# Latent queries from six column blocks, with the rotated rows carried to their heads

## The chip, the cores and the metric

One Trainium2 chip, one of its cores. The metric is the device time of one execution in microseconds (us). The kernel before took 927.07 us, the median of three runs (926.96 to 927.24).

## The reference, cut to what matters

One layer of an encoder on 512 tokens of width 1024: a SwiGLU block, a mixer, a SwiGLU block, each between RMS norms. The mixer runs neighbourhood attention (8 heads of 64) and latent attention (8 heads) over one input projection. The change touches the latent attention's queries and keys alone:

```python
q = (rms_norm(c_q, q_norm_g) @ w_uq).reshape(B, S, H, 64 + 32)
q_nope, q_rot = jnp.split(q, [64], axis=-1)
q_rot = apply_rope(q_rot, cos, sin)      # x1*cos - x2*sin, x2*cos + x1*sin
k_rot = apply_rope(k_rope, cos, sin)     # one key part, shared by the heads
s = (q_nope . k_nope + q_rot . k_rot) * 96 ** -0.5
```

The latent `c_q` has 256 columns, so a query product contracts over two blocks of 128. Each head has 64 columns without position and 32 with it, the latter in two halves x1 and x2 of 16.

## The kernel before

All products run as three matmuls over float32r halves: `mm3` (line 353) takes hi.hi, hi.lo and lo.hi, where `split` (line 333) makes hi by a copy on ACT (ScalarE) and lo by a subtraction on DVE (VectorE), or on POOL (GpSimd) where that is asked for. PE is TensorE, SP is SyncE, which issues most DMAs in the order of the program; POOL issues a few.

The whole layer is written as calls that only collect operations (`Plan`, line 44). `issue` (line 220) then orders all of them, for all engines, once at build time, from costs and due times that `add` and `place` hold, and writes them out in that order. So on the chip each engine has a fixed order, and a wait holds up what stands behind it on its engine.

The mixer's part that matters here, in the order of the source:

- `na_pair` (line 996) does the neighbourhood attention for two heads at a time; its output stands in `ov`, the right half of `h[1]`, its values V in columns 8192 to 12287 of the big region.
- `latent(n)` (line 1085) makes the latents of token tile n, normalises them and builds the rotated key. In columns 384 to 511 of `cb[n]` stand the products with cos, the products with sin, and their sum twice (line 1108). `latent_T` (line 1110) transposes the tile, and `split` writes `cT`; its block 3 has the rotated key in rows 64 to 127, twice the same 32 rows.
- `q_weights(u)` (line 1142) loads the query weights of four heads into a raw buffer of 1024 columns: per head and block 64 + 32 columns and the 32 with position once more with their halves exchanged, by three DMAs. `q_head(hd)` (line 1149) makes a head's query as one product with 128 columns, so the array is full: 64 rows without position, 32 rotated, 32 exchanged. One DVE multiplication by `tbl` (line 1157) puts the scale on the first 64 rows, scale x cos on the next 32 and scale x sin with its signs on the last 32; `split` then writes the query's place (`Q_AT`, line 931). Each score's product with the doubled key rows adds the two parts.
- `k_pair(j)` (line 1178) makes the keys without position of two heads, `rope_rows(hd)` (line 1170) carries rows 64 to 127 of the rotated key to the buffers of heads 1 to 7 by DMAs within SBUF, issued by POOL.
- `mla_pair(j, hf)` (line 1187) does the attention of two heads for half of the tokens: scores, row minima on DVE, exponentials on ACT, transposes, a split into the probability buffers `pts` (line 1227: two of 2048 columns at 8192 and 10240, where V stood), products with the values. `w_out_a` (line 1230), the output projection of the neighbourhood half, is PE work that the plan may put in between.

PSUM has eight banks; `prep` (line 1081) hands out banks 0 to 5 in turn to the transposes, value, query and key products. The scores then use banks 0 and 1, the transposes 2 and 3 (line 1225). Raw weights have three buffers (line 285), split weights four (lines 286 and 287), both used in turn: the query weights of the two halves and the four of w_out's first half follow each other in them.

Of the kernel before, what the change touches and what calls it, by code (L numbers as in the profile page):

```python
# [14 lines left out]
AF = mybir.ActivationFunctionType  # L15
ALU = mybir.AluOpType
AX = mybir.AxisListType

P = 128
D = 1024  # L20
S = 512
# [6 lines left out]
EPS = 1e-6  # L28
NH = 8
TAIL = 3  # L30


class Ring:
# [10 lines left out]
class Plan:  # L44
# [3 lines left out]
    ahead, margin = 250, 0  # L48
    TAIL = {"ACT": 95, "DVE": 75, "POOL": 45, "PE": 176}
    LAG = {"ACT": 60, "DVE": 50, "POOL": 85, "PE": 120, "SP": 60}  # L50
# [60 lines left out]
    def add(self, eng, op, a, k):  # L111
# [16 lines left out]
        in_sb = sum(kind(x) != "psum" for x in big)  # L128
        tail, lock, dma = self.TAIL.get(eng, 0), False, 0
        if op == "dma_start":  # L130
# [111 lines left out]
def r_(ap):  # L242
    return ap.bitcast(F32R)
# [3 lines left out]
def hybrid_block(ctx, tc, A, out):  # L247
    nc = tc.nc
    plan = Plan(tc)
    ACT, DVE, POOL, PE, SP = (plan.engine(e) for e in ("ACT", "DVE", "POOL", "PE", "SP"))  # L250
# [13 lines left out]
    def bank(i, n=512):  # L264
        return psum[:, i * 512 : i * 512 + n]
# [31 lines left out]
    gbs = Ring([gbuf[:, :1024], gbuf[:, 1024:]])  # L297
    hall = new(4096)
    h = [hall[:, n * 1024 : (n + 1) * 1024] for n in range(NT)]
    tbl = h[3][:, 512:]  # L300
    mask = h[2][:, 512:768]
    tts = [new(1024)]
    R0 = at[1]
# [1 line left out]
    def reg(o, n):  # L305
        assert R0 + o + n <= NCOL - N32
        return mem[:, R0 + o : R0 + o + n]
# [25 lines left out]
    def split(dst_hi, dst_lo, src, eng=DVE):  # L333
        ACT.copy(r_(dst_hi), src)
        n = src.shape[-1]
        for c in [slice(i, i + 512) for i in range(0, n, 512)] if eng is POOL else [slice(0, n)]:
            eng.tensor_tensor(r_(dst_lo[..., c]), src[..., c], dst_hi[..., c], ALU.subtract)
# [6 lines left out]
    def load_w(src, n=1024, eng=DVE, raw=None, to=None):  # L344
        raw = fetch(src, n) if raw is None else raw
        hi, lo = to or (his.get()[:, :n], los.get()[:, :n])
        split(hi, lo, raw, eng)
        return hi, lo
# [4 lines left out]
    def mm3(ps, a, b, start, stop):  # L353
        mm(ps, a[0], b[0], start, False)
        mm(ps, a[0], b[1], False, False)
        mm(ps, a[1], b[0], False, stop)
# [37 lines left out]
    def ffn(w_gu, w_dn, gpost, on_tile, L, first, resid, mid_tile=None, rs=None):  # L394
# [134 lines left out]
        c0, n_pairs, n_first = L["pairs"]  # L529
        plain = [c for c in range(NFC - TAIL) if not c0 <= c < c0 + 2 * n_pairs]  # L530
        three = [reg(L["slots"][0], 1024), his.items[3], los.items[3]]
        slots = {c: three[i % 3] for i, c in enumerate(plain)}
        slots |= {c: reg(o, 1024) for c, o in zip(range(NFC - TAIL, NFC), L["slots"][1:])}
        w_to = {c: (his.items[i % 4], los.items[i % 4]) for i, c in enumerate(plain)}
# [262 lines left out]
    for k in range(KD):  # L797
        o = sq.get() if k else acc
# [14 lines left out]
    v = [x.rearrange("p (n t) -> p n t", n=NT) for x in (sq.items[0], bank(3))]  # L813
# [65 lines left out]
    def nb():  # L879
        return prb.get()  # L880
# [11 lines left out]
    for n in range(NT):  # L892
        ps = bank(2 * n)
# [37 lines left out]
    Q_AT = (7168, 5120, 18432, 19456, 20480, 4096, 6144, 25600)  # L931
# [27 lines left out]
    def o_rstd(g, ns):  # L959

        b = bank(trb.get(), 8)
        w = 2 * len(ns)
        for i, v in enumerate((sqs[g], sqr)[: g + 1]):
            for n, t in enumerate(ns):
                PE.matmul(b[:, 2 * n : 2 * n + 2], v[:, t * P : (t + 1) * P], ones, start=i + n == 0,
                          stop=i == g, skip_group_check=True)
        s = stat.get()[:, :w]
        DVE.tensor_scalar(s, b[:, :w], 1.0 / 512, EPS, ALU.mult, ALU.add)
        r = ors[g][:, 2 * ns[0] : 2 * ns[0] + w]
        POOL.tensor_tensor(r, s, nhalf.to_broadcast([P, w]), ALU.pow)  # L970
        return ors[g][:, ::2]
# [94 lines left out]
    qk_pair(2)  # L1066
    na_pair(2)
    qk_pair(3)
    SP.dma_start(tbl, A["tbl"])
    SP.dma_start(tokt.rearrange("p n c -> p (n c)"), A["tokt"])  # L1070
    na_pair(3)
    rA = o_rstd(0, range(NT))


    gc = (gbuf[:, 1792:], h[2][:, 768:896])
    v = A["g_c"]
# [4 lines left out]
    prep = Ring(list(range(6)))  # L1081
    cT = reg(14336, 4096).rearrange("p (a b t) -> p a b t", a=2, b=4)
    cTh = [cT[:, 0, i, :] for i in range(4)]
    cTl = [cT[:, 1, i, :] for i in range(4)]
    def latent(n):
        ps = bank(nb(), 416)
        for k in range(KD):
            w = [a.rearrange("p (k c) -> p k c", k=2)[:, k % 2, :] for a in wc[k // 2]]
            mm3(ps, xt(k, n * P, (n + 1) * P), w, k == 0, k == KD - 1)
        s = stat.get()  # L1090
        ACT.activation(cb[n][:, :256], ps[:, :256], AF.Square, scale=1.0 / 16, accum_out=s[:, 0:1])
        ACT.activation(cb[n][:, 256:384], ps[:, 256:384], AF.Square, scale=128.0 ** -0.5, accum_out=s[:, 1:2])
        DVE.tensor_scalar(s[:, 2:4], s[:, 0:2], EPS, None, ALU.add)
        r = stat.get()
        POOL.tensor_tensor(r[:, 0:2], s[:, 2:4], nhalf.to_broadcast([P, 2]), ALU.pow)
        r1, r2 = r[:, 0:1], r[:, 1:2]
        c = cb[n]
        DVE.scalar_tensor_tensor(c[:, 0:256], ps[:, 0:256], r1, gc[0], ALU.mult, ALU.mult)
        DVE.scalar_tensor_tensor(c[:, 256:384], ps[:, 256:384], r2, gc[1], ALU.mult, ALU.mult)
        tk = tokt[:, n, :]  # L1100
        DVE.tensor_tensor(c[:, 384:416], ps[:, 384:416], tk[:, 0:32], ALU.mult)
        v = ps[:, 400:416]
        v = bass.AP(tensor=v.tensor, offset=v.offset, ap=[v.ap[0], [-16, 2], [1, 16]])
        DVE.tensor_tensor(c[:, 416:448].rearrange("p (a c) -> p a c", a=2), v,
                          tk[:, 32:64].rearrange("p (a c) -> p a c", a=2), ALU.mult)
        v = [bass.AP(tensor=x.tensor, offset=x.offset, ap=[x.ap[0], [0, 2], [1, 32]])
             for x in (c[:, 384:416], c[:, 416:448])]
        DVE.tensor_tensor(c[:, 448:512].rearrange("p (a c) -> p a c", a=2), v[0], v[1], ALU.add)

    def latent_T(n):  # L1110
        b = bank(prep.get())
# [10 lines left out]
    raw = raws.get()  # L1122
# [16 lines left out]
    Q = {}  # L1139
    wq = {}  # L1140

    def q_weights(u):
        raw = raws.get()
        to, src = raw.rearrange("p (i c) -> p i c", i=8), A["w_uq"][u].rearrange("p (i c) -> p i c", i=8)
        for o, c0, c1 in ((0, 0, 96), (96, 80, 96), (112, 64, 80)):
            SP.dma_start(to[:, :, o : o + c1 - c0], src[:, :, c0:c1])
        wq[u] = [x.rearrange("p (k h c) -> p k h c", k=2, h=4) for x in load_w(None, raw=raw)]

    def q_head(hd):
        hi, lo = wq[hd // 4]  # L1150
        i = hd % 4
        ps = bank(prep.get())
        for k in range(2):
            mm3(ps, (hi[:, k, i, :], lo[:, k, i, :]), (cTh[k], cTl[k]), k == 0, k == 1)
        q = reg(Q_AT[hd], 1024)
        Q[hd] = (q[:, :512], q[:, 512:])
        DVE.tensor_tensor(ps, ps, tbl, ALU.mult)
        split(q[:, :512], q[:, 512:], ps)

    q_weights(0)  # L1160
    q_weights(1)
    for hd in range(NH):
        q_head(hd)
    kbuf = [(cTh[3], cTl[3])]
    for o in range(4):
        m = reg(21504 + 1024 * o, 1024)
# [222 lines left out]
```

## Time and profile before

| | |
|---|---|
| median of three runs | 927.07 us (926.96 to 927.24) |
| the profiled execution, its own time | 926.21 us |
| its span, first to last instruction | 924.1 us |
| mean granted TensorE clock | 0.998 of full |
| PE busy | 914.2 us, 99% of the span |
| DVE busy | 813.0 us, 88% |
| ACT busy | 544.1 us, 59% |
| POOL busy | 357.3 us, 39% |

The profile is of one execution. Busy times are sums over an engine's instructions, so they say how full an engine is over the whole span, not which one sets the time of a stage. PE counts as busy while a matmul's modelled length runs, and matmuls overlap; the distance between starts is the better measure of what one costs. Nearly every operation is written out by line 238, at the end of the planner, so a line tells nothing; operations are told apart by engine, shape and place in time. `m` is ordinary SBUF, `memr` the float32r region.

### The profile page before, as it was taken

Reading aid. Unit: us, or ns where it says so; the run is one execution under the profiler, and the core shown is the slowest. Engines: PE = TensorE matmul, PEld = TensorE weight load, DVE = VectorE, ACT = ScalarE, POOL = GpSimd, SP = SyncE. Lnnn points to the kernel's source line nnn. Section 1 sums busy time; section 2 is a strip of 40 time slices with the busy share of each in tenths; the row PEclk is TensorE's granted clock in tenths of the full one; section 3 lists DMA queues with packets and bytes.
Section 4 is the critical chain, followed back from the end, with each engine's and each line's share of the span. In section 5 each row is a group of like instructions: output and inputs, shape, how many; then the busy total and the mean of one; then the engine's idle time right before and its main releaser. Section 6 shows DMA issues by size and latency. Waiting matters only on the chain. (4 is left out here: it accounts for less than half of the span.)

```text
span 924.1 us, 15672 instructions
## 1 busy us (share of the span) xinstructions
PE 914.2 (99%) x5822; PEld 826.6 (89%) x5822; DVE 813.0 (88%) x1205; ACT 544.1 (59%) x972; POOL 357.3 (39%) x300
## 2 busy tenths in 40 slices
PE   9999999999999999999999999999999999999996
PEld 7889999999887788888978888999999999988785
DVE  7999999899999896588796678999998989999986
ACT  7446544544675674588777867655544444458562
POOL 0005777860300313222552323238787665130040
PEclk9999999999999999999999999999999999999999
DMA  7535354446534496314290115244434445464324
GB/s 259 171 114 183 115 145 142 158 124 221 171 126 149 114 268 181 63 57 93 93 190 26 46 46 180 94 171 162 144 119 144 131 126 180 142 208 145 114 69 159
DMA packets 65932, 128.02 MB, mean 139 GB/s; under 512 B 22337, under 2 KB 32449, under 8 KB 65857
## 3 DMA queue, kind: packets, MB, share of 16 engines
q1 hardware_dynamic: 64704, 125.20, 43.5%
q0 software_dynamic: 1008, 1.84, 1.2%
q8 instruction: 45, 0.74, 0.3%
q14 instruction: 31, 0.25, 0.1%
q10 hardware_dynamic: 144, 0.00, 0.0%
HBM read 107.36 MB, written 17.83 MB: 135 GB/s over the span
## 5 line engine op out<-in xcount | busy, mean ns | idle before, releaser
L238 PE MATMUL psum<-memr 128*128 128x256 f32 (+3 forms) x5480 | 894.0, 323 | 0.7 <-ACT memr L238 0.2
L238 PEld LDWEIGHTS psum<-memr 128*128 128x128 f32 x5480 | 788.4, 190 | 79.9 <-DVE memr L238 3.8
L238 POOL TENSOR_TENSOR m<-m 128x512 f32<-128x512 f32 (+7 forms) x255 | 318.1, 1263 | 491.5 <-DVE m L238 201.8
L238 ACT CAST memr<-m 128x1024 fp32r<-128x1024 f32 (+3 forms) x388 | 304.5, 811 | 223.8 <-PE psum L238 91.4
L238 DVE TENSOR_TENSOR memr<-m,memr 128x1024 fp32r<-128x1024 f32 (+4 forms) x379 | 405.0, 1098 | 17.8 <-ACT memr L238 16.9
L238 DVE TENSOR_TENSOR m<-psum,m 128x512 f32<-128x512 f32 (+4 forms) x199 | 125.0, 632 | 32.9 <-ACT m L238 22.6
L238 DVE TENSOR_TENSOR m<-m 128x512 f32<-128x512 f32 (+3 forms) x179 | 101.2, 589 | 3.6 <-DMA m<-in_ffn_w_down 0.5
L238 ACT CAST memr<-psum 128x512 fp32r<-128x512 f32 (+2 forms) x124 | 63.6, 522 | 31.2 <-PE psum L238 22.5
L238 DVE TENSOR_TENSOR memr<-psum,memr 128x512 fp32r<-128x512 f32 (+3 forms) x116 | 67.9, 603 | 12.5 <-ACT memr L238 11.3
L238 ACT COPY m<-psum 128x512 f32<-128x512 f32 (+3 forms) x98 | 45.4, 474 | 37.0 <-PE psum L238 34.6
L238 PE MATMUL psum<-m 128*128 128x128 f32 (+1 forms) x342 | 54.6, 279 | 2.1 <-DVE m L238 2.0
L238 DVE TENSOR_TENSOR psum<-psum,m 128x256 f32<-128x256 f32 (+1 forms) x86 | 49.9, 585 | 4.7 <-PE psum L238 3.1
L238 PEld LDWEIGHTS psum<-m 128*128 128x128 f32 x342 | 43.6, 155 | 10.0 <-DVE m L238 2.2
L238 ACT ACTIVATE m<-m 128x256 f32<-128x256 f32 (+3 forms) x88 | 41.4, 475 | 11.7 <-DVE m L238 11.5
L238 ACT ACTIVATE m<-psum 128x256 f32<-128x256 f32 (+2 forms) x62 | 27.4, 443 | 27.2 <-DVE psum L238 15.0
L238 DVE SCALAR_TENSOR_TENSOR m<-m 128x512 f32<-128x512 f32 (+1 forms) x36 | 32.2, 934 | 3.7 <-POOL m L238 3.2
L238 ACT ACTIVATE m<-psum,m 128x512 f32<-128x512 f32 x40 | 26.9, 687 | 7.7 <-DVE m L238 5.8
L238 POOL TENSOR_TENSOR memr<-m,memr 128x512 fp32r<-128x512 f32 (+1 forms) x14 | 23.2, 1673 | 14.1 <-ACT memr L238 7.7
L238 ACT ACTIVATE memr<-m 128x512 fp32r<-128x512 f32 (+2 forms) x28 | 20.9, 757 | 13.1 <-DVE m L238 11.6
L238 DVE TENSOR_REDUCE m<-psum 128x1 f32<-128x512 f32 x32 | 21.2, 682 | 2.0 <-PE psum L238 1.9
L238 ACT COPY psum<-m 128x512 f32<-128x512 f32 x28 | 16.3, 589 | 10.3 <-DVE m L238 10.0
L238 POOL CAST memr<-memr 64x512 fp32r<-64x512 f32 x8 | 5.9, 739 | 35.6 <-DVE memr L238 34.2
(26 smaller groups left out, 99.1 us busy)
## 6 DMA issues: line engine op xcount, KB each, us to landing
m<-in_ffn_w_gu SPq DMA_DIRECT2D x86, 512.0 KB
m<-in_ffn_w_down SPq DMA_DIRECT2D x44, 512.0 KB
gd<-m SPq DMA_DIRECT2D x44, 256.0 KB
m<-gd SPq DMA_DIRECT2D x64, 128.0 KB
m<-in_w_qk SPq DMA_DIRECT2D x8, 512.0 KB
h<-m SPq DMA_DIRECT2D x8, 512.0 KB
m<-in_w_out SPq DMA_DIRECT2D x8, 512.0 KB
m<-h SPq DMA_DIRECT2D x8, 512.0 KB
```

The lines of the kernel that those rows point to most:

```text
L238: r = getattr(self.engines[eng], op)(*a, **k)
```

## The change

- The query weights are loaded in another order, by two DMAs for each half of the heads: first the columns without position, 64 per head and block, then those with position, 32 per head and block; 768 columns, nothing doubled.
- `q_heads(u)` makes the queries of four heads from three column blocks of 128: one block holds the columns with position of all four heads, the two others those without position of two heads each. So there are six blocks in place of eight.
- The block with position is multiplied by cos (`cos4`) and by sin (`sin4`), each to a bank of its own, both are split into a spare region (columns 8192 to 12287, the later `pts`), and sixteen DMAs on SP carry 32 rows each to rows 64 to 95 and 96 to 127 of the heads' queries.
- The blocks without position are scaled on their way out of PSUM: ACT writes hi with the scale, DVE lo in one fused operation, over 64 rows per head.
- The exchange of the halves is now done on the key: the sum of the two products is written once, and a small DVE copy writes its exchanged form beside it.
- The table of 128 rows gives way to two: cos, repeated four times by one DMA, and sin, by eight DMAs of 16 rows into the right half of `h[1]`, after `na_pair(3)`.

```diff
+Q_SCALE = -(96.0 ** -0.5)
...
-    tbl = h[3][:, 512:]
+    cos4, sin4 = h[3][:, 512:], h[1][:, 512:]
...
-    SP.dma_start(tbl, A["tbl"])
+    v = A["tbl"]
+    SP.dma_start(cos4, bass.AP(tensor=v.tensor, offset=v.offset + 64 * S, ap=[[0, 4], [S, 32], [1, S]]))
     SP.dma_start(tokt.rearrange("p n c -> p (n c)"), A["tokt"])
     na_pair(3)
+    for i in range(8):
+        o = (112, 96)[i % 2] * S
+        SP.dma_start(sin4[16 * i : 16 * i + 16], bass.AP(tensor=v.tensor, offset=v.offset + o, ap=[[S, 16], [1, S]]))
...
-        v = [bass.AP(tensor=x.tensor, offset=x.offset, ap=[x.ap[0], [0, 2], [1, 32]])
-             for x in (c[:, 384:416], c[:, 416:448])]
-        DVE.tensor_tensor(c[:, 448:512].rearrange("p (a c) -> p a c", a=2), v[0], v[1], ALU.add)
+        DVE.tensor_tensor(c[:, 448:480], c[:, 384:416], c[:, 416:448], ALU.add)
+        v = c[:, 496:512]
+        v = bass.AP(tensor=v.tensor, offset=v.offset, ap=[v.ap[0], [-16, 2], [1, 16]])
+        DVE.tensor_copy(v, c[:, 448:480].rearrange("p (a c) -> p a c", a=2))
...
     def q_weights(u):
         raw = raws.get()
-        to, src = raw.rearrange("p (i c) -> p i c", i=8), A["w_uq"][u].rearrange("p (i c) -> p i c", i=8)
-        for o, c0, c1 in ((0, 0, 96), (96, 80, 96), (112, 64, 80)):
-            SP.dma_start(to[:, :, o : o + c1 - c0], src[:, :, c0:c1])
-        wq[u] = [x.rearrange("p (k h c) -> p k h c", k=2, h=4) for x in load_w(None, raw=raw)]
+        src = A["w_uq"][u].rearrange("p (i c) -> p i c", i=8)
+        for o, c0, c1 in ((0, 0, 64), (512, 64, 96)):
+            SP.dma_start(raw[:, o : o + 8 * (c1 - c0)].rearrange("p (i c) -> p i c", i=8), src[:, :, c0:c1])
+        wq[u] = load_w(None, 768, raw=raw[:, :768])
-    def q_head(hd):
...
+    def q_heads(u):
+        for i in range(4):
+            q = reg(Q_AT[4 * u + i], 1024)
+            Q[4 * u + i] = (q[:, :512], q[:, 512:])
+        def product(o, step):
+            ps = bank(prep.get())
+            for k in range(2):
+                mm3(ps, [x[:, o + step * k : o + step * k + P] for x in wq[u]], (cTh[k], cTl[k]), k == 0, k == 1)
+            return ps
+        ps, p2 = product(512, P), bank(prep.get())
+        DVE.tensor_tensor(p2, ps, sin4, ALU.mult)
+        DVE.tensor_tensor(ps, ps, cos4, ALU.mult)
+        for a, x in enumerate((ps, p2)):
+            m = reg(8192 + 2048 * u + 1024 * a, 1024)
+            split(m[:, :512], m[:, 512:], x)
+            for i in range(4):
+                q = reg(Q_AT[4 * u + i], 1024)
+                SP.dma_start(q[64 + 32 * a : 96 + 32 * a], m[32 * i : 32 * i + 32])
+        for j in range(2):
+            ps = product(P * j, 256)
+            for e in range(2):
+                hi, lo = (x[0:64] for x in Q[4 * u + 2 * j + e])
+                x = ps[64 * e : 64 * e + 64]
+                ACT.activation(r_(hi), x, AF.Copy, scale=Q_SCALE)
+                DVE.scalar_tensor_tensor(r_(lo), x, Q_SCALE, hi, ALU.mult, ALU.subtract)
...
-    for hd in range(NH):
-        q_head(hd)
+    for u in range(2):
+        q_heads(u)
```

## Rows read from the trace of the kernel before

**Rows 1.** The page: its span, and its first part, busy time by engine.

```profile
span 924.1 us, 15672 instructions
...
PE 914.2 (99%) x5822; PEld 826.6 (89%) x5822; DVE 813.0 (88%) x1205; ACT 544.1 (59%) x972; POOL 357.3 (39%) x300
```

**Rows 2.** Windows: length; busy PE, PEld, DVE, ACT, POOL (instructions); PE clock; DMA share; GB/s.

```profile
460.00:480.00 20.00, 20.00 (x89) 15.94 (x88) 18.62 (x30) 14.21 (x24) 13.18 (x14) 1.00 0.90 186
480.00:540.00 60.00, 59.98 (x366) 51.48 (x366) 43.69 (x82) 48.15 (x106) 18.74 (x19) 1.00 0.18 57
540.00:600.00 60.00, 58.79 (x389) 52.43 (x388) 49.90 (x71) 39.24 (x73) 16.62 (x17) 1.00 0.33 115
800.00:924.10 124.10, 116.79 (x533) 95.47 (x531) 108.21 (x170) 68.36 (x112) 22.85 (x33) 0.98 0.41 131
466.50:474.00 7.50, 7.50 (x35) 6.21 (x34) 7.29 (x13) 5.31 (x9) 2.68 (x3) 1.00 1.17 191
```

**Rows 3.** Waits of PE, whole span: total us, times, longest.

```profile
PE psum L238 <- DVE m L238: 2.0, 3, 1.1
```

**Rows 4.** Timeline of DVE from 463.9 to 485: start, length (both us), what.

```profile
463.96 0.69 DVE L238 TENSOR_TENSOR psum<-psum,m 128x512 f32<-128x512 f32 x1
...
465.91 1.29 DVE L238 TENSOR_TENSOR psum<-psum,m 128x512 f32<-128x512 f32 x2
...
480.06 1.28 DVE L238 TENSOR_REDUCE m<-psum 128x1 f32<-128x512 f32 x2
```

**Rows 5.** Groups by shape, 457.5 to 481.5: count | busy us, mean ns | idle before.

```profile
L238 PE MATMUL psum<-memr 128*128 128x512 f32 x101 | 24.2, 397 | 0.0
...
L238 DVE TENSOR_TENSOR memr<-psum,memr 128x512 fp32r<-128x512 f32 x16 | 10.4, 682 | 0.9 <-ACT memr L238 0.7
L238 ACT CAST memr<-psum 128x512 fp32r<-128x512 f32 x15 | 8.8, 587 | 6.3 <-DVE psum L238 4.7 <-PE psum L238 1.2
L238 DVE TENSOR_TENSOR psum<-psum,m 128x512 f32<-128x512 f32 x8 | 5.4, 693 | 0.1
```

**Rows 6.** Timeline of PE from 464.0 to 475.8: start, length, what.

```profile
463.66 12.40 PE L238 MATMUL psum<-memr 128*128 128x512 f32 x54
```

**Rows 7.** Groups by shape, whole span.

```profile
L238 DVE SCALAR_TENSOR_TENSOR memr<-psum,memr 64x512 fp32r<-64x512 f32 x8 | 5.5, 688 | 7.9 <-ACT memr L238 7.7
...
L238 ACT ACTIVATE memr<-psum 64x512 fp32r<-64x512 f32 x8 | 4.7, 591 | 7.7 <-PE psum L238 7.6
```

**Rows 8.** Timelines of DVE around 450.2 to 464: start, length, what.

```profile
450.80 0.69 DVE L238 TENSOR_TENSOR m<-m 128x512 f32<-128x512 f32 x1
...
454.59 0.28 DVE L238 TENSOR_TENSOR m<-psum,m 128x32 f32<-128x32 f32 x2
454.90 0.35 DVE L238 TENSOR_TENSOR m<-m 128x64 f32<-128x64 f32 x1
```

**Rows 9.** Instructions of two inputs: ns least/median/most, first and last start.

```profile
L238 SPq DMA_DIRECT2D m<-in_w_uq x6: 540/600/1125, 422.3 to 433.4; - x6
...
L238 SPq DMA_DIRECT2D m<-in_tokt x1: 328/328/328, 10.0 to 10.0; - x1
```

**Rows 10.** POOL's key carries: issues of 462 to 467, 474 to 480, all seven's landing.

```profile
memr<-memr POOLq DMA_DIRECT2D x4, 256.0 KB, 7.3
...
memr<-memr POOLq DMA_DIRECT2D x3, 256.0 KB, 3.6
...
DMA to landing us min/median/max: 3.0/6.4/8.0
```

**Rows 11.** Timeline of POOL from 460 to 482: start, length, what [idle before].

```profile
464.84 1.79 POOL L238 DMA_DIRECT2D memr<-memr  x3
...
474.79 1.26 POOL L238 DMA_DIRECT2D memr<-memr  x2 [3.39 <-PE psum L238]
476.34 2.54 POOL L238 TENSOR_TENSOR memr<-m,memr 128x512 fp32r<-128x512 f32 x2 [0.30 <-ACT memr L238]
```

**Rows 12.** Timeline of ACT from 474 to 487: start, length, what.

```profile
486.63 0.59 ACT L238 CAST memr<-psum 128x512 fp32r<-128x512 f32 x1
```

More of the change, by code (lines that the diff above doesn't have):

```diff
@@ L1143, in q_weights @@
         raw = raws.get()
-        to, src = raw.rearrange("p (i c) -> p i c", i=8), A["w_uq"][u].rearrange("p (i c) -> p i c", i=8)
-        for o, c0, c1 in ((0, 0, 96), (96, 80, 96), (112, 64, 80)):
-            SP.dma_start(to[:, :, o : o + c1 - c0], src[:, :, c0:c1])
-        wq[u] = [x.rearrange("p (k h c) -> p k h c", k=2, h=4) for x in load_w(None, raw=raw)]
-    def q_head(hd):
[L1150 to L1158, printed above, removed]
+        src = A["w_uq"][u].rearrange("p (i c) -> p i c", i=8)
```

## The prediction

> **What bounds the kernel.** I read the page's busy line first [rows 1]: TensorE (PE) is busy in 914.2 of 924.1 us, far ahead of VectorE (DVE) with 813.0 and ScalarE (ACT) with 544.1. The windows say where that could be otherwise [rows 2]: PE fills 20.00 of 20 us from 460 to 480, where the queries are made, and 59.98 of 60 from there to 540, most of the latent attention. The longest entry among PE's own waits is 2.0 us in three pieces [rows 3]. So an instruction that PE need not run is worth its full time, as long as nothing new makes PE wait. The second reading decides about that: in 460 to 480 DVE is busy in 18.62 of 20 us and the DMA engines have a share of 0.90, while in 480 to 540 DVE has 43.69 of 60 and the DMA engines 0.18 [rows 2]. DVE's eight multiplications by the table mark the query work (psum from psum and m, 128x512); they begin at 463.96 us, and the first row minima of the latent scores, at 480.06, end the stage [rows 4].
>
> The sum is made against the profiled execution: span 924.1, its own time 926.21, so 2.1 us lie outside the span. The median of the three runs is 927.07, 0.86 more; I add that at the end.
>
> **Fewer products.** Before, eight heads x two blocks x three terms are 48 matmuls of 128x512; after, two halves x three column blocks x six are 36. One costs PE its pitch, not its 397 ns of modelled length [rows 5]: 54 of them in a row take 12.40 us [rows 6], so (12.40 - 0.40) / 53 = 0.2265 us. Twelve fewer: **-2.72 us**. Their weight loads run beside other matmuls and are counted at nothing.
>
> **Emptying PSUM.** Before, DVE has 8 multiplications at 693 ns and 8 subtractions at 682: 11.0 us. After, 4 and 4 of these (5.5) and 8 fused ones over 64 rows, which exist in the first attention's queries at 688 (5.5) [rows 5, 7]: 11.0, the same. ACT goes from 8 casts at 587 (4.7) to 4 of them and 8 scaled copies at 591 (7.1) [rows 5, 7]: 2.4 us more, in a stretch where it is busy in 14.21 of 20 [rows 2]; nothing. Without that cover it would be 2.4. The two weight splits shrink from 1024 to 768 columns, a few tenths on DVE and ACT, which I don't count.
>
> **The keys' exchange.** Per tile the add shrinks from 64 to 32 columns (0.35 us, [rows 8]) and a copy over 32 columns joins it; the pair over 32 columns beside it takes 0.28 for two [rows 8]. Three tiles are hidden; for the last, whose transposes gate all queries, I take **+0.1 us**, between 0 and 0.2.
>
> **Tables.** The sine rows go where the first attention keeps its output until 451.5 (the DVE product at 450.80, 0.69 long, [rows 8]). Eight issues on SP (SyncE) at 0.33 us, like the token table's [rows 9], end at 454.1; the shortest landing of a carry inside SBUF is 3.0 [rows 10]: 457.1, and the first multiplication stands at 463.96. Nothing, with 6.9 us of cover; even the longest landing, 8.0, leaves 1.9.
>
> **SP's queue.** It loses six w_uq issues (0.54, 0.66 and 1.13 per half, [rows 9]) and the table's (at 0.33), 5.0 us; it gains four w_uq (at most 2.6), the cosine, eight sine and sixteen carries at 0.33, 8.3. The net of 5.9 us is spread over the 30 us from 450, in which SP is mostly waiting. A carry waits on SP for its split; behind it stand only the later w_out loads, whose products come after 540. Nothing.
>
> **The carries.** This is the term that the trace doesn't show. Sixteen transfers of 32 rows x 4 KB, 2.10 MB in all, from the regions that later are the two probability buffers (line 1227) to rows 64 to 127 of the queries. First half: two multiplications from 463.96 (start to start 0.60: two take 1.29, one 0.69, [rows 4]), cast and subtraction, so the first transfer is issued near 466.0 and the eighth by 468.7; the second half follows 2.6 later, until 471.5. The nearest rows are the seven key carries, 256 KB each, issued by GpSimd (POOL): 3.0, 6.4 and 8.0 us at least, in the median and at most [rows 10]; the first four take 7.3 in the median, the last three 3.6. The fourth is issued at 466.0 (three from 464.84 on, 0.6 apart, [rows 11]), so it lands near 473.3, and from 466.5 to 474 the DMA engines' share is 1.17 at 191 GB/s [rows 2]: full. The new 2.10 MB queue with them; at 191 GB/s they add 11.0 us, so everything has landed by 473.3 + 11.0 = 484.3. The need: heads 0 and 1 read their queries shortly before the minima at 480.06, and their transfers are the first in the queue. The binding one is the second buffer, first written when head 1's probabilities are split, at 486.63 in the trace [rows 12] and 2.7 earlier after the saving: 483.9. So **+0.4 us** of ACT waiting, passed on to PE; ends: 0 (idle engines take them at once) and 6.2 (rival two). I take 0.4 because the 191 GB/s row is the one in which SBUF carries and weight loads mix as they will here.
>
> Sum: -2.72 + 0.1 + 0.4 = -2.2; 926.21 - 2.2 = 924.0 for a profiled execution, 927.07 - 2.2 = **924.9** for the median. Own range 924.3 (no wait) to 925.2. About 0.2%, 1.85 us, is what a measurement of this kernel can tell from no change, so this case counts as faster.
>
> **Rival one: VectorE sets the pace, nothing is gained.** The first scores need banks 0 to 3, which the queries and keys must have left; DVE has 24 jobs there before and after (8 + 8 + 8 of the keys, against 8 + 8 + 8), and 18.62 of 20 us are full [rows 2]. If PE has nothing else for the 2.7 us, it idles: 927.1. For it: the fill, w_out's first half, waits for weight buffers that the query weights leave late; POOL splits the last of them at 476.34 [rows 11]. Against it: those 8 x 12 products are 21.7 us of PE work that may stand anywhere up to 540, and DVE is idle in 16 of the 60 us after 480.
>
> **Rival two: the carries come late, slower.** Place: ACT's first write to the second probability buffer; until the second half's eight transfers have read it, ACT stands, behind it the exponentials and casts of head 1, and PE runs dry. Price: two late key carries, issued from 474.79 and landed about 3.6 after the second issue at 475.4, moved 0.52 MB in 4.2 us, 125 GB/s [rows 10, 11]. From 473.3 on, 2.10 MB then take 16.8 us, until 490.1, 6.2 after the need: 927.07 - 2.6 + 6.2 = 930.7. It decides from 2.6 us late, a landing at 486.5. For it: the full DMA share; the order is fixed at build time and cannot react. Against it: at that pace without the backlog they land at 482.8, in time. The Trainium skill (SBUF — State Buffer, Door 1: The DMA port swizzle (why `[64,N]` ≈ `[32,N]`)) states 189 GB/s for 1 MiB over 32 partitions, since these reach 8 of 16 ports; by that figure the landing would be an estimated 484.4, 0.5 late, and the sum an estimated 925.0, so this rival would fall. The trace's full stretch agrees with 191, its pair of 64-row carries with 125 doesn't.
>
> **Rival three: the order elsewhere moves.** The list of all instructions is ordered anew, also from 540 to 600 and after 800, where PE isn't full (58.79 of 60 and 116.79 of 124.1, [rows 2]): 1.2 us are lost in the first. The same again, gained or lost on top of the forecast: 923.7 to 926.1, and up to 2 more from a changed end.
>
> **Numbers.** Forecast 0.48, rival one 0.22, rival two 0.18, rival three 0.12. Faster: the forecast and a third of rival three, 0.52. Within 0.2%: rival one, a third of rival two (little lateness) and a third of rival three, 0.32. Slower: 0.16. The range begins a little under rival three's lower end, 923.5, and takes in rival two up to 929.2, a lateness of 4.7; about 0.17 is left out.
>
> **What would show it.** Right: 12 fewer matmuls of 128x512, four table multiplications where there were eight, eight fused splits over 64 rows, PE full from 460 to 540, the first row minima no later than 480, ACT's wait on a DMA under 1 us, the span near 922. Rival one: PE idle, released by DVE or ACT, before the first scores. Rival two: ACT or PE released by a DMA from memr to memr, and carries that land 10 us or more after their issue. Wrong altogether: a time under 923.5, or PE waits far from this stage.

## The result, and the profile after

The changed kernel takes **935.76 us** in the median (932.99 to 936.39, four runs) against 927.02 of the kernel before (926.54 to 927.24): a ratio of 1.0091, interval 1.0079 to 1.0103, 8.74 us slower. The forecast was 924.9, the range ended at 929.2. The profiled execution took 936.39, its span is 934.6.

The page's first part, beside [rows 1]: PE runs twelve matmuls fewer and is busy 3.3 us longer.

```profile
span 934.6 us, 15702 instructions
...
PE 917.5 (98%) x5810; PEld 825.4 (88%) x5810; DVE 813.6 (87%) x1209; ACT 545.4 (58%) x976; POOL 355.9 (38%) x300
```

The windows of [rows 2] and two around the longest stall (columns as there):

```profile
460.00:480.00 20.00, 19.10 (x83) 13.84 (x81) 19.18 (x33) 15.76 (x31) 14.39 (x15) 1.00 0.94 237
480.00:540.00 60.00, 55.62 (x312) 46.97 (x313) 39.17 (x72) 43.19 (x92) 16.41 (x17) 0.94 0.37 81
540.00:600.00 60.00, 59.42 (x374) 52.15 (x373) 48.70 (x75) 40.60 (x80) 19.09 (x20) 1.00 0.35 115
...
493.20:496.60 3.40, 0.01 (x1) 0.01 (x1) 1.35 (x3) 0.55 (x1) 0.00 (x0) 0.89 0.51 118
496.60:502.60 6.00, 6.00 (x22) 5.21 (x23) 2.25 (x4) 2.40 (x6) 0.00 (x0) 0.50 0.00 0
```

PE was full from 460 to 540; now it lacks 0.9 us before 480 and 4.4 behind it. From 493.2 to 496.6 it does nothing, and the six microseconds that follow run at a granted clock of 0.50, the lower of its levels (1.2 GHz): 22 matmuls and transposes, where the same stretch of the kernel without the stall holds 37 (first experiment).

Who is waited for: the first line is among DVE's waits, the others are PE's, of the whole span (of before: [rows 3]).

```profile
DVE memr L239 <- DMA memr<-memr: 4.1, 1, 4.1
...
PE psum L239 <- DVE memr L239: 5.1, 4, 3.5
PE psum L239 <- DVE m L239: 3.2, 4, 1.1
```

The timelines of DVE (first the row minima that end the stage, at 480.06 in [rows 4]; then the place of the stall), and of SP's issues:

```profile
482.94 0.69 DVE L239 TENSOR_REDUCE m<-psum 128x1 f32<-128x512 f32 x1
...
488.78 0.68 DVE L239 TENSOR_REDUCE m<-psum 128x1 f32<-128x512 f32 x1
490.31 0.18 DVE L239 RECIPROCAL m<-m 128x4 f32<-128x4 f32 x1 [0.85 <-ACT m L239]
490.70 0.42 DVE L239 TENSOR_TENSOR m<-psum,m 64x256 f32<-64x256 f32 x1 [0.21 <-ACT m L239]
495.25 1.29 DVE L239 TENSOR_TENSOR memr<-psum,memr 128x512 fp32r<-128x512 f32 x2 [4.13 <-DMA memr<-memr]
...
471.81 4.62 SPq L239 DMA_DIRECT2D memr<-memr  x6
476.53 0.52 SPq L239 DMA_DIRECT2D m<-in_w_out  x1
477.09 4.02 SPq L239 DMA_DIRECT2D memr<-memr  x6
481.22 1.83 SPq L239 DMA_DIRECT2D m<-in_w_out  x1
483.50 3.25 SPq L239 DMA_DIRECT2D memr<-memr  x4
486.85 0.53 SPq L239 DMA_DIRECT2D m<-in_w_out  x1
```

The instruction that waits is DVE's subtraction for the low half of head 1's probabilities. It writes the second half of the second probability buffer, where the second half's sine rows wait to be carried away. Those four carries were issued from 483.50 to 486.75, behind twelve others and two weight loads, and DVE got the buffer at 495.25. That is rival two, one instruction further on: ACT's write to the first half, which the cosine rows had held, went through.

Of the signs that the prediction named, the counts came true (twelve matmuls fewer, four multiplications, eight fused splits). The stage itself is late before any buffer is waited for: the first row minima of the latent scores begin at 482.94, 2.9 us after those of before.

### The profile page after: what moved, and what is told of

Same layout as the page of the kernel before. It is cut to its first block, busy times and chain, and to the rows that moved or that the text cites. A ratio compares the mean times of both kernels' runs of the same rounds, so it can differ in the third digit from the quotient of the medians.

```text
span 934.6 us, 15702 instructions
## 1 busy us (share of the span) xinstructions
PE 917.5 (98%) x5810; PEld 825.4 (88%) x5810; DVE 813.6 (87%) x1209; ACT 545.4 (58%) x976; POOL 355.9 (38%) x300
## 5 line engine op out<-in xcount | busy, mean ns | idle before, releaser
L239 POOL TENSOR_TENSOR m<-m 128x512 f32<-128x512 f32 (+6 forms) x255 | 318.1, 1263 | 483.6 <-DVE m L239 157.5
L239 DVE TENSOR_TENSOR memr<-m,memr 128x512 fp32r<-128x512 f32 (+5 forms) x379 | 403.6, 1094 | 23.0 <-ACT memr L239 22.0
L239 DVE TENSOR_TENSOR memr<-psum,memr 128x512 fp32r<-128x512 f32 (+2 forms) x112 | 65.1, 600 | 15.9 <-ACT memr L239 10.8
L239 ACT CAST memr<-psum 128x512 fp32r<-128x512 f32 (+2 forms) x120 | 60.8, 521 | 27.7 <-PE psum L239 21.6
L239 DVE TENSOR_TENSOR psum<-psum,m 128x256 f32<-128x256 f32 (+1 forms) x82 | 47.1, 580 | 4.7 <-PE psum L239 3.1
```

The costliest lines, as they stand in the source:

```text
L239: r = getattr(self.engines[eng], op)(*a, **k)
```

## The experiments

Three theories stood against each other: the **hold** (rival two: late carries keep the probability buffer), the **full DMA engines** (called rival A below: another transfer would be waited for in its place), and **VectorE's pace** (rival B: the work that empties PSUM sets the time, so TensorE's saving is worth nothing). "The same order" means that the list of all instructions, as the plan had written it for the named kernel, was put into the kernel as constants, so that an edit moves nothing else. The kernel before was timed again beside every group of runs; its median stands with a run's result where it isn't 926.8. The diffs are cut to what matters (`...`), and orders are written in words.

### The hold

```diff
-split(m[:, :512], m[:, 512:], x)
+m = (m[:, :512], m[:, 512:])
+if u and a:
+    m = (cb[0], cb[1])      # left halves of h[0], h[1]
+split(m[0], m[1], x)
...                          # the carries read from the same two places
```

> The changed kernel with its instructions in the very same order on every engine; only the split buffer of the second half's sine rows lies in two column stretches that nobody writes before 500 us, in place of the second half of the second probability buffer. Theory (the late carries hold that buffer, VectorE's write to it waits 4.1 us, TensorE stands 3.6 us and then runs 6.8 us at the lower clock): VectorE's wait on the carries goes, TensorE's stall at 492.7 us and the stretch at clock 0.5 go with it, 935.8 becomes 929.5 to 930.5. Rival A (the DMA engines are full from 466 to 495 us, so that another wait for a transfer takes the place of this one): at most 1.5 us faster, 934 to 936. Rival B (the engines' extra work on 64 rows sets the pace): the stall shrinks but the next stretch fills up, 932.5 or more.

Measured: **930.25** (ratio to before 1.0040, 1.0028 to 1.0052), 5.5 us faster than the changed kernel. Its windows:

```profile
493.20:496.60 3.40, 3.40 (x24) 2.95 (x23) 1.61 (x4) 3.10 (x8) 0.00 (x0) 1.00 0.58 117
496.60:502.60 6.00, 6.00 (x37) 4.89 (x36) 4.66 (x10) 4.69 (x11) 3.37 (x3) 1.00 0.26 89
460.00:480.00 20.00, 19.18 (x84) 13.89 (x81) 19.16 (x33) 15.84 (x31) 14.46 (x15) 1.00 0.92 237
480.00:540.00 60.00, 59.12 (x351) 50.39 (x352) 44.75 (x82) 49.00 (x106) 18.64 (x19) 1.00 0.39 81
```

The stall and the stretch at half clock are gone and nothing took their place. Of the 5.5 us the idle 3.4 is one part, the clock the other, an estimated 2.1. The changed kernel's own runs put the clock a little higher: three with a mean clock of 0.994 to 0.996 took 935.74 to 936.39, the one with 0.999 took 932.99, 2.8 less than the median (its stall was not profiled).

The same hold from the other end, with the buffers left where they were:

```diff
 order of SP: ... carries (cosine, half 2)
-w_out block 1 (second set), w_out block 2
 carries (sine, half 2)
+w_out block 1 (second set), w_out block 2
```

> The changed kernel in its own order but for two instructions: SP's loads of the second and third w_out block of the second set (issued at 476.5 and 481.2 us, 512 KB each) come behind the last carry. The split buffers stay where they were. Theory (the carries are late because they stand in SP's queue behind 1 MB of weights and 2.3 us of issuing): the last carry lands at 489 to 491 us in place of 495, VectorE's wait falls under 0.5 us, 929.5 to 931. Rival A (the DMA engines are full with keys and carries alone, whatever the order in SP's queue): it lands at 493 or later and at most 2 us come back, 933.5 to 936. If a weight block then comes too late for ScalarE's copy of it, ScalarE waits on a load near 492 us and TensorE with it.

Measured: **930.79** (1.0034 to 1.0058). DVE no longer waits for a carry. SP's queue, with nothing between the carries, and the write to the buffer on DVE:

```profile
472.50 12.52 SPq L410 DMA_DIRECT2D memr<-memr  x16
485.13 2.40 SPq L410 DMA_DIRECT2D m<-in_w_out  x3
...
492.01 1.40 DVE L410 TENSOR_TENSOR memr<-psum,memr 128x512 fp32r<-128x512 f32 x2 [0.19 <-ACT memr L410]
```

So 1 MB of weights ahead in the queue was enough to turn a carry in time into one that is 4 us late. The last issue ends only 1.7 us earlier than in the changed kernel (485.02 against 486.75), and the buffer is free at least 3.2 earlier (492.01 against 495.25); so part of the gain is in the transfers themselves, which no longer wait behind the weights. With the buffers apart and the order planned anew:

> The same move of the sine rows' split buffer, with the order left to the planner, which no longer sees a hold on the probability buffer. Theory: like the run with the fixed order or better, 928 to 931; the 4 to 5 us that the changed kernel loses before 482 us (stalls at 447.6, 464.2 and 479.5 us) are the planner's order and may come out another way. Rival A: 934 to 936.

Measured: 930.93 (1.0044 to 1.0069), the same, with stalls of 0.3, 0.8 and 1.1 us between 464 and 482. So the rest doesn't come from an order that was planned around the hold; a new plan, which sees no hold, comes out as late.

### What is left: 3.4 us, and 2.7 that should have come

With the hold gone the kernel is still slower than before. Two of the stalls were moved one at a time, in the order of the run with the buffer apart:

```diff
 PE: ... latent 1, -transposes of tile 0 (three), latent 2, latent 3, +transposes of tile 0 ...
```

> The run with the buffer apart, in the same order but for three TensorE instructions: the first three transposes of the first latent block come behind the fourth block's products, beside the fourth transpose. Theory (TensorE waits 1.3 us at 447.6 us for a block that it could take later): 1.0 to 1.4 us faster than the run with the buffer apart, 928.9 to 929.3. Rival B (VectorE paces what follows, so that TensorE only waits later): no change, 930 to 930.5, with the 1.3 us added to stalls between 460 and 482 us.

Measured: 930.68 (before 926.51), no gain. PE now waits 1.60 us for DVE at the same place, for the next block's products.

```diff
 ACT, DVE: keys of head 0, +head 1, head 2, ... 7, -head 1
```

> The run with the buffer apart, in the same order but for two instructions: the split of the second head's keys comes on ScalarE and VectorE ahead of the splits of heads 3 to 7 in place of behind them. Theory (the stall of 1.2 us at 479.4 us is TensorE waiting for this split alone): the stall shrinks to under 0.3 us, 929.0 to 929.5. Rival B (VectorE is late by as much with everything): another stall released by VectorE takes its place before 490 us, 930 to 930.5.

Measured: **932.82** (before 926.51), 2.6 slower, outside both ranges. ACT's copy of the second head's keys reads the bank that DVE also reads for the first head; ACT stood 0.73 us until DVE was done, and everything behind it came later. PE's stall grew from 1.05 to 2.17 us, and the granted clock was 0.72 on the mean of the next six. PE without and with the edit:

```profile
480.88 4.39 PE L410 MATMUL psum<-memr 128*128 128x512 f32 x18 [1.05 <-DVE memr L410]
...
483.13 6.00 PE L410 MATMUL psum<-memr 128*128 128x512 f32 x18 [2.17 <-DVE memr L410]
```

The 1.1 us of stall and the 1.6 that the eighteen matmuls took longer make up the 2.6. In both runs moving one item made another wait, as rival B has it.

Then the whole order by hand. All instructions that both kernels share come in the order of the kernel before, on top of the buffer apart:

```diff
-order of the plan for six blocks
+order of the plan for eight blocks; product 1 to 6 in the slots of heads 0 to 5
```

> The changed kernel with the sine rows' buffer apart, and with an order written out by hand: every instruction that both kernels have comes in the order of the kernel before, on every engine; the six products stand where the first six of the eight heads' products stood, the two blocks with position first and third, their emptying in VectorE's and ScalarE's old slots. Theory (besides the hold, what the change lost is the order that came out around it: stalls of 1.3, 1.2 and three times 0.3 to 0.6 us between 447 and 482 us, and some 1.4 us between 340 and 420): these go, the 2.7 us of the twelve matmuls come out, 924 to 926. Rival B (the work on VectorE has grown and paces the stage whatever the order): 928 or more, with stalls released by VectorE between 463 and 486 us.

Measured: 929.37 (1.0018 to 1.0040; before 926.51), 0.9 faster than with the plan's order, and not the 924 to 926 of the theory. The same with the sine rows back in the probability buffer:

> The hand-written order of the first run of this group, with the sine rows' split buffer where the change put it, in the second probability buffer. Theory (with the order of before the second half's carries start some 5 us earlier, and one w_out load stands between the carries and the buffer's first write instead of two): the wait is under 1 us, 924 to 926.5, within 0.7 us of that run. Rival A (the transfers are too slow for the place of the buffer in any order): VectorE waits 2 us or more for a carry before 495 us, 928 or more.

Measured: 929.18 (before 926.51; 1.0021 to 1.0043), no wait on a carry. The carries didn't start 5 us earlier, as the theory had it: they were issued from 469.78 to 485.35, with one w_out load between them where the changed kernel has two. So the place of the buffer cost time only in the order with both loads ahead.

Three further edits on the hand-written order (in the diff P0 and P1 are the first half's two blocks without position, e0 and e1 a block's two heads, sin and cos the multiplications, ss and sc the splits of their results):

```diff
-cosine rows by one DMA of stride zero, sine rows by eight DMAs
+SP.dma_start(cos4, A["tbl"][0:P]); SP.dma_start(sin4, A["tbl"][P : 2 * P])
...
-DVE.tensor_copy(v, ...)      # the exchange
+ACT.copy(v, ...)
...
-DVE: ... P0e0 P0e1 sin1 cos1 P1e0 ss1 sc1 P1e1 ...
+DVE: ... P0e0 P1e0 P0e1 sin1 cos1 P1e1 ss1 sc1 ...   (ACT and PE accordingly)
```

> The hand-written order with three further edits: the two tables lie in HBM as they are used, so that each is one load of 128 rows (the change reads the cosine rows four times over with a stride of zero, and the sine rows in eight loads); the exchange's small copy goes from VectorE to ScalarE; and the emptying of a bank's two heads is interleaved with another bank's, so that VectorE and ScalarE do not wait for each other's turn at one bank. Theory (in the first hand-written order VectorE lost 0.55 us to five waits on the sine loads, 1.2 us to the copy beside a POOL instruction and some 2 us to the turns, and the cosine load delayed a weight block at 364 us): 925.5 to 927.5. Rival B (VectorE and ScalarE pace the stage in any order): 928 or more.

Measured: **926.87** (before 926.58; ratio 1.0003, 0.9994 to 1.0012): no difference from the kernel before. The tables alone, in the order of the run with the buffer apart:

> The run with the buffer apart, in the same order, with the tables alone altered: each is one load of 128 rows. Theory (the cosine rows read four times over delay the weight block that lands at 368.5 us in place of 364.3, which costs 0.6 to 1.1 us at 370 us and 0.45 at 401; the seven extra sine loads cost VectorE 0.5 us of waits before its first product): 928.5 to 929.3. Rival (these stalls come and go from run to run and the waits lie beside others): 929.8 to 930.5.

Measured: 930.59 (before 926.58), no gain, though the stall at 370 us is gone in its trace. So the tables cost nothing that can be measured, as forecast, and the 2.5 us between the two hand-written orders came from the copy and the interleaving; how much from which, no run here shows. And the carries themselves:

> The first kernel of this group with the sixteen carries left out, so that the heads' rows with position hold whatever lay there. Theory (once no buffer is held, the carries lie beside other work): within 0.5 us of the first kernel of this group. Rival A (their 2 MB and SP's issuing delay keys and w_out blocks that are waited for): 1 us faster or more.

Measured: 926.75 (before 926.58), 0.1 from the run with the three edits. Sixteen carries that nobody waits for cost nothing that can be measured, and rival A falls.

### Where the twelve matmuls went

One stall of 2 us was left in the hand-written order; it was put down to one ACT copy.

```diff
 ACT: ... +copy of w_out block 3, last query copies, keys of heads 2, 0, 4, 3, -copy of w_out block 3 ...
```

> The hand-written order with the tables and the copy altered, and one ScalarE instruction moved: the copy of the fourth w_out block comes ahead of the second half's last query copies and the key copies, into a gap of 1.1 us that ScalarE has at 471.4 us. Theory (the 2.1 us that TensorE still stands at 473.9 us is this one copy, queued behind copies that wait their turn at a bank): the stall falls under 0.5 us, 924.8 to 925.6, faster than both kernels. Rival B (ScalarE and VectorE pace the stage, the copies pushed back will be waited for next): 926 or more, with a stall of 1 us or more released by ScalarE or VectorE before 485 us.

Measured: 927.63 (before 926.75; 1.0003 to 1.0021), not faster. The timelines of PE in the two kernels:

```profile
468.70 5.53 PE L409 MATMUL psum<-memr 128*128 128x512 f32 x22
476.21 2.10 PE L409 MATMUL psum<-memr 128*128 128x512 f32 x8 [1.97 <-ACT memr L409]
```

```profile
469.64 5.53 PE L409 MATMUL psum<-memr 128*128 128x512 f32 x22
477.16 2.13 PE L409 MATMUL psum<-memr 128*128 128x512 f32 x8 [1.99 <-DVE memr L409]
```

The stall kept its length and its place in PE's order; only its releaser changed, from ACT to DVE, and a second one of 0.69 us, released by ACT, came up at 489.36. Doubling the products with position puts twelve matmuls back, without any other work:

```diff
-for k in range(2):
+for k in (0, 1) * rep:      # rep = 2 for the blocks with position
```

> The first kernel of this group with each product with position computed twice, twelve matmuls of 128x512 more, which is what the change removed; at the pitch of 0.2265 us they are 2.72 us of TensorE. Theory of the forecast (TensorE paces the stage, the twelve matmuls count in full): 2.2 to 2.8 us more than the first kernel of this group. Rival B (VectorE and ScalarE pace the stage, so that TensorE's shorter work was worth nothing there): under 0.8 us more.

Measured: 928.40 (before 926.58), 1.5 more than the run with the three edits, between both expectations. In the order of the run with block 3 earlier:

> The first kernel of this group with the products with position computed twice, twelve matmuls of 128x512 more (2.72 us at the pitch). In the order before this one they cost 1.5 us, between both expectations. Theory (what hid 1.2 us of them there was the stall at 473.9 us): they now cost 2.2 to 2.8 us. Rival B (the other engines pace it): under 1.6 us.

Measured: 929.44 (before 926.75), 1.8 more, again between both. But this number holds a fall of the clock. PE without and with the twelve:

```profile
477.16 5.06 PE L409 MATMUL psum<-memr 128*128 128x512 f32 x20 [1.99 <-DVE memr L409]
...
479.14 6.43 PE L410 MATMUL psum<-memr 128*128 128x512 f32 x20 [1.97 <-DVE memr L410]
479.20:485.40 6.20, 6.20 (x20) 4.85 (x21) 4.08 (x7) 3.40 (x7) 2.38 (x1) 0.72 1.21 208
```

The stall of 2 us is as long as before and comes 2 us later; the granted clock is 0.72 behind it (the last line is a window), and the same twenty matmuls take 1.4 us longer. Five of the eight executions have a mean clock of 0.995 or 0.996 and took 929.09 to 930.33; the other three took 928.19, 928.23 and 929.35. So this pair of runs doesn't settle what twelve matmuls are worth. These kernels also differ from the one before in much, so the last pair starts from the kernel before itself, in its own order:

```diff
...
-mm3(ps, (hi[:, k, i, :], lo[:, k, i, :]), (cTh[k], cTl[k]), k == 0, k == 1)
+if hd < 6:
+    mm(ps, hi[:, k, i, :], cTh[k], k == 0, False)
+    mm(ps, hi[:, k, i, :], cTl[k], False, k == 1)
+else:
+    mm3(...)
```

> The kernel before in its own order, with twelve matmuls of 128x512 left out of the queries (the third one, weights' low part times latents' high part, of each half of heads 0 to 5); nothing else is altered, so that it shows what the change's first term is worth by itself. Theory of the forecast (TensorE paces this stage): 2.3 to 2.8 us faster than the kernel before. Rival B (VectorE's chain from the first query product to the second head's keys paces it, and TensorE's full row of before only just covers that chain): under 1.2 us faster, with TensorE standing 1.5 us or more between 464 and 485 us.

Measured: **926.05** (before 926.58; ratio 0.9996, 0.9987 to 1.0005). Twelve matmuls fewer, nothing gained that can be measured. Window, and the timelines of PE, ACT and DVE:

```profile
460.00:480.00 20.00, 18.13 (x78) 13.86 (x77) 18.79 (x31) 14.28 (x24) 13.32 (x15) 1.00 0.90 188
...
463.72 6.05 PE L408 MATMUL psum<-memr 128*128 128x512 f32 x26
470.60 4.37 PE L408 MATMUL psum<-memr 128*128 128x512 f32 x18 [0.82 <-DVE memr L408]
476.01 5.32 PE L408 MATMUL psum<-memr 128*128 128x512 f32 x21 [1.04 <-ACT memr L408]
...
471.78 3.23 ACT L408 CAST memr<-psum 128x512 fp32r<-128x512 f32 x6 [1.36 <-DVE psum L408]
474.92 1.04 ACT L408 CAST memr<-m 128x1024 fp32r<-128x1024 f32 x1
...
479.76 1.28 DVE L408 TENSOR_REDUCE m<-psum 128x1 f32<-128x512 f32 x2
```

PE falls from 20.00 to 18.13 of 20 us; DVE stays at 18.79 (18.62 in [rows 2]), and the first row minima come 0.3 us earlier than before, at 479.76. PE's second stall ends with ACT's copy of a block of w_out (474.92, 1.04 long), the very work that could have filled PE's time: it stands in ACT's list behind casts that wait for DVE's multiplications. The second of the pair relieves DVE:

```diff
-DVE.tensor_tensor(ps, ps, tbl, ALU.mult)
```

> The kernel just before this one with VectorE's eight multiplications of the queries by the table left out too (8 by 0.6 us of VectorE between 463 and 480 us). Rival B: with VectorE relieved the twelve matmuls count, 2.2 to 2.8 us faster than the kernel before. If something else holds the stage (the keys' carries, ScalarE): no more than 0.5 us faster than the kernel just before this one.

Measured: **923.29** (before 926.58; ratio 0.9967, 0.9955 to 0.9980), 3.3 faster than before, half a microsecond more than the 2.2 to 2.8 expected. Its window, and the first row minima, 2.1 us earlier than before: PE is full again, DVE has 3.6 us to spare.

```profile
460.00:480.00 20.00, 19.98 (x92) 15.72 (x91) 16.41 (x26) 16.01 (x28) 15.74 (x16) 1.00 1.02 213
...
477.92 1.28 DVE L408 TENSOR_REDUCE m<-psum 128x1 f32<-128x512 f32 x2
```

So DVE's chain from the first product to the keys, with the casts on ACT that wait for it, paces the stage once PE has less to do. PE's full row of before covered that chain with hardly anything over: both were near the limit. Two things weren't tried: DVE relieved with all 48 matmuls kept, and the shorter products in another order of the kernel before.

### The exchange

The exchange on the keys alone, eight blocks of queries kept; first planned anew, then in the order of before, then with the copy on ACT.

```diff
-DVE.tensor_tensor(c[:, 448:512]..., ALU.add)
+DVE.tensor_tensor(c[:, 448:480], ..., ALU.add)
+DVE.tensor_copy(c[:, 480:512], halves exchanged)      # last run: ACT.copy
...                          # table and query weights loaded to match, in other pieces
```

> One part alone on the kernel before: rotation's exchange is moved to the keys (with the tables and weights arranged for it), queries stay in eight blocks of 128 rows, no carries. Theory (the latent stage's stall at 447.6 us in the changed kernel comes from the order chosen there, not from the exchange itself): 926.5 to 928. Rival C (the exchange's fourth small VectorE instruction per block, 1.27 us where it meets POOL, lengthens the latent stage whatever else is done): 928.3 or more.

Measured: 927.97 (1.0005 to 1.0022), the upper edge of the theory's range; it doesn't decide.

> The exchange moved to the keys alone, on the kernel before, with every instruction in the order of the kernel before (the earlier run of this part was planned anew and came out 1.2 us slower). Theory (the fourth small instruction meets POOL's subtraction and takes 1.2 us in place of 0.2, and the last latent block's products wait for it): 927.2 to 928.2, a stall of 0.5 us or more at 461 us. Rival (it was the new order): 926.3 to 927.

Measured: **927.84** (before 926.75; 1.0005 to 1.0023), 1.1 slower, with a stall of 0.71 us released by DVE at 461.2. Its timeline of POOL and DVE there:

```profile
458.55 3.77 POOL L408 TENSOR_TENSOR memr<-m,memr 128x512 fp32r<-128x512 f32 x3
...
459.58 0.30 DVE L408 TENSOR_TENSOR m<-m 128x32 f32<-128x32 f32 x1
459.92 1.19 DVE L408 COPY m<-m 128x32 f32<-128x32 f32 x1
```

> The kernel just before this one with the exchange's copy issued by ScalarE in place of VectorE, in the same place of the order. Theory (the collision with POOL is what costs): no stall over 0.2 us at 461 us, 926.2 to 927, 0.5 to 1 us faster than the run before it. Rival (the copy's chain costs on any engine, or nothing does): within 0.3 us of it.

Measured: 927.13 (before 926.75; 0.9995 to 1.0013), 0.7 faster than the run before it, no stall there. The copy on ACT:

```profile
460.98 0.22 ACT L408 COPY m<-m 128x32 f32<-128x32 f32 x1
```

## Why the prediction was wrong

**Fewer products, -2.72: the step that set the sign.** The count and the pitch were right. That they lie on the path was read from PE being busy 20.00 of 20 us, and that doesn't say that PE paces. The run that takes only these matmuls out gains 0.5 us, within its interval nothing; relieving DVE too gives 3.3. That is **rival one's** mechanism, and its time, 927.1, is what the best version with six blocks takes (926.87). I held against it that w_out's products may stand anywhere up to 540 and that DVE is idle later. The order is fixed, though: PE meets the first scores where they stand in its list, w_out's blocks are copied by the same ACT that waits for DVE, and DVE's idle time behind 480 is no use to a chain that must end before.

**The carries, +0.4: measured +5.5, the clock included.** This is rival two's mechanism. It priced the wait at 6.2; DVE waited 4.1 and PE 3.5. Its time, 930.7, was too low all the same, because it took the 2.6 from the matmuls for granted and left out the clock. The rate was not the error: from 470 to 496 the changed kernel's DMA engines moved

```profile
DMA packets 2114, 5.34 MB, mean 206 GB/s; under 512 B 413, under 2 KB 413, under 8 KB 2111
```

all transfers together, which is near the 191 that I took. The prediction's figure from the Trainium skill (SBUF — State Buffer, Door 1: The DMA port swizzle (why `[64,N]` ≈ `[32,N]`)), 189, is the page's for 1 MiB over 32 partitions; no run here shows such a transfer by itself, so the figure wasn't tested, and its estimate of 925.0 fell with mine. What failed is what I had standing ahead of the last carry. I had it issued by 471.5; its issue ended at 486.75, 15.3 later. The first was issued at 471.81 in place of 466.0: 5.8, of which 5.1 are the multiplications, which began at 469.11 in place of 463.96. Sixteen issues took 0.78 us each where nothing stood between them (12.52 in the run with the loads last) and not the 0.33 of a table load [rows 9]: 7.2. POOL's three carries in [rows 11], 0.6 apart, were the nearer row. Two w_out loads stood between: 0.52 + 1.83 = 2.4. Together 15.4. "A carry waits on SP for its split; behind it stand only the later w_out loads" looked at who waits behind a carry, and not at what a carry waits behind, though the kernel before has five w_out loads in SP's list from 460.89 to 482.96:

```profile
460.89 22.07 SPq L238 DMA_DIRECT2D m<-in_w_out  x5
```

The need moved too, from 483.9 to 491.1 (end of DVE's 490.70 instruction), or the loss would have been larger. With the late issues alone the carries were still in time (the run with the loads last); the two w_out loads, which also moved 1 MB ahead of the last carries, made them too late.

**The clock.** That a stall of 3.4 us brings 6 us at half clock was not in the price; it makes an estimated 2.1 to 2.8 of the 5.5.

**The keys' exchange, +0.1: measured +1.1** (on the kernel before, in its order). I priced the copy by instructions that didn't meet POOL. 0.7 of it goes with the copy to ACT; the 0.4 left is within the interval.

**Emptying PSUM, Tables.** Tables: right, nothing (the run with the tables alone). Emptying: DVE's sum is the same, as forecast (813.6 busy against 813.0). What the sum leaves out is that ACT and DVE took turns at the two heads of a bank; one such wait was read here, the 0.73 us at the keys; what they cost together is not shown.

**Rival three, the order elsewhere, 1.2 at most.** The order within the stage cost more: 8.74 less the hold (5.5) and the exchange (1.1), and with the 0.5 of the matmuls, leaves 2.6, if these parts add up, which no run shows. The hand-written order with the copy on ACT wins back 3.4 from the run with the buffer apart, of which 0.7 may be the copy's: 2.7, nearly the same. How it divides among single stalls stays open; moving them one by one gave nothing.

The range failed because the rivals were given chances as if one excluded the others. Here the mechanisms of all three were at work together.

No version here beats the kernel before. The best with six blocks equals it (926.87 against 926.58), and more would need less of DVE between the first product and the keys; that was only tried by leaving its work out.

## What to carry to other kernels

An engine that is full paces a stage only if it stays full when its neighbour's work stays and its own shrinks. Look for a second engine that is nearly as full in the same window (here DVE with 18.62 of 20 us), and take work out of the first by itself before the change is built. For a buffer lent to transfers, count from the issue of the last one, with the queue's loads ahead of it and its issue time taken from transfers of the same kind. And price rivals that can be true together by their sum.

## What the runs showed of the hardware that was not expected

- A DVE copy of 128x32 within SBUF takes 0.18 us while POOL stands still (at 459.31 in the changed kernel) and 1.27 (at 463.84) where POOL began a subtraction over 512 columns at 463.79; both end at 465.1. The same copy on ACT takes 0.22. The Trainium skill (SBUF — State Buffer, SBUF: two separate sides) says that VectorE and GpSimd take a shared pair of ports by turns, the first for its whole instruction; the trace agrees.
- SP needs 0.59 us in the median to issue one carry of 32 rows x 4 KB within SBUF, up to 1.39 (0.78 each over sixteen in a row), against 0.33 to 0.38 for the four w_out loads of 512 KB that the changed kernel issues from 458 to 467.
- The clock fell to the lower level after PE had stood 3.46 us (the changed kernel), 2.17 us (second head's keys first) and 1.97 us (twelve matmuls put back, in the second order). It did not in the profiles of the run with the three edits and of the one with block 3 earlier, after 1.97 and 1.99: a stall of 2 us came with either.
- Reading the same 32 rows of HBM four times over for the cosine table held up a weight block behind it: ACT began on the block at 368.5 us, against 365.8 with a table of 128 rows in the same order and 364.3 before. It cost nothing that can be measured here.
